# A hybrid decoder block: the two ends of its feed-forward stage rearranged

## The chip, the cores and the metric

The kernel runs on one core of one Trainium2 chip. The metric is device time in microseconds of one execution, as a median over runs. Five engines of the core appear in the profile: PE (TensorE, matmuls) with PEld (its weight loads), DVE (VectorE), ACT (ScalarE), POOL (GpSimd) and SP (SyncE, which here only issues DMAs).

## What is computed

One decoder layer on x of 512 tokens by 2048 features, all in float32. Two token mixers (block-sparse attention and a state-space group) give `mixed` (512 x 2048); then

```
x = x + mixed @ w_out                       # w_out 2048 x 2048
h2 = rms_norm(x, norm2_gain)                # x * rsqrt(mean(x^2) + eps) * gain, per token
ff = square(relu(h2 @ w_ff1))               # w_ff1 2048 x 8192
x = x + ff @ w_ff2                          # w_ff2 8192 x 2048
```

The change touches the passage from `w_out` to the feed-forward stage and that stage itself.

## The kernel before, in words

**Split products.** Each float32 operand is used as a sum of two float32r parts, high and low: ScalarE casts to the high part (`S.copy`), VectorE subtracts it from the operand (`V.tensor_sub`) for the low part. A product then takes three matmuls per tile (low x high, high x low, high x high), each 128 x 128 weights by 512 columns. Weights come by DMA on SP's queue in 512 KB loads.

**End of `w_out` (lines 802 to 824).** `panel` computes 512 output columns (a quarter, n = 0 to 3) for all four token tiles m into four PSUM banks. VectorE adds each bank, scaled, to x1[m] (line 809); ScalarE squares the result into a temporary and keeps the sum (`ssq2`, line 811). Then the quarter is transposed, 4 x 4 transposes into banks `ht` (line 819), and `scaled_split` (lines 183, 184) makes the pair h2h[n], h2l[n], without the per-token factor. After quarter 3, `rsqrt_mean` (lines 168 to 179, a chain of 14 small VectorE operations) makes that factor `rstd2`, and `token_bcast` (lines 186 to 194) spreads it over a 128 x 512 tile `rbc` by four copies `tbw` and a product with the identity into bank `tb`. `rbc` is first read in `ff1`'s eviction (line 872).

**Buffers.** `early` holds the pools of weights `wp` (28 KB per partition), temporaries `tmp` (12 KB) and PSUM `psm` (four banks for panels, one `ax`) and the three banks for transposes. They are closed at line 829; the pools opened next, `ff` in SBUF and `pff` with all eight PSUM banks, lie on the same addresses, and each of their tiles waits only for the tiles that lay there (`reuse_waits="tile"`). In `ff` are, in this order, 7 raw weight tiles of 4 KB per partition, 3 `th`, 3 `tl` of 4 KB, 9 left factors `lf` of 4 KB and 3 temporaries `ls` of 2 KB.

**The feed-forward loop (lines 849 to 986).** The 8192 hidden columns are 16 blocks b of 512. `ff1(b, r)` is the first product, a generator of 32 steps: two halves hf of 256 hidden columns, 16 steps k each, six matmuls `f` a step (lines 864 to 866); every fourth step loads and splits one `w1` tile (lines 845, 846). Step k reads h2h[k // 4]. At the end of a half VectorE applies relu and `rbc`, ScalarE squares (lines 872, 873). `left(r)` makes from r the seven left factors of a Strassen-Winograd product with two-by-two quarters a11, a12, a21, a22 (first index: token half, second: hidden half hf, so a11 and a21 come from hf = 0): each factor a cast and a subtraction (lines 884, 885), with sums s1 to s4 between. `ff2(b, lf)` is the second product: two column halves n of 1024 outputs, seven products of 12 matmuls `g` each (lines 930 to 934) in the order 1, 5, 6, 2, 7, 3, 4; each splits its right operand (line 846), which before products 5, 6, 7, 4 VectorE makes in place (lines 945, 949, 955, 961), and adds its bank to x1 (line 940). Banks X, Y, Z carry running sums over several products. In the last block the 16 output DMAs of line 967 follow.

**What sets the order.** The loop interleaves by hand: after each product of `ff2(b)` two or three steps of `ff1(b + 1)` are written, `drain(f1, 2 + (i % 7 in (1, 4)))`, 16 for each n, so that in each n one hf passes; in the last block there is no `ff1`. Ahead of the loop `drain(ff1(0, r))` runs alone. The framework (`schedule_with_timeline_sim=True`) then orders each engine's instructions from the written order, from `hi()` (high priority: splits, evictions, x1 additions) and from a timeline of its own; an engine works through its instructions in that order. SP's queue is such an order too: a load waits for a free raw tile, and what is queued behind it waits as well.

Of the kernel before, what the change touches and what calls it, by code (L numbers as in the profile page):

```python
# [45 lines left out]
def hybrid_block_kernel(ctx, tc, x, norm1_gain, w_in, q_norm_gain, k_norm_gain,  # L46
# [26 lines left out]
    def ax(name):  # L73
        return psm.tile([P, 512], F32, name=name, tag="ax", bufs=1)
# [13 lines left out]
    def tq(name, shape=(P, 512)):  # L88
        return tmp.tile(list(shape), F32, name=name, tag="tq", bufs=4)
# [93 lines left out]
        S.activation(dh, src, AF.Copy, scale=gain)  # L183
        V.scalar_tensor_tensor(dl, src, gain, dh.bitcast(F32), op0=ALU.mult, op1=ALU.subtract)

    def token_bcast(dst, col4):

        ps = ax("tb")
        for m in range(4):
            w = tq("tbw", (P, P))  # L190
            V.tensor_scalar(w, col4[:, m:m + 1].to_broadcast([P, P]), 1.0, None,
                            op0=ALU.mult)
            PE.matmul(ps[:, m * P:(m + 1) * P], w, ident, start=True, stop=True)
        V.tensor_copy(dst, ps)
# [606 lines left out]

    ssq2 = const.tile([P, 4, 4], F32, name="ssq2")
    h2h, h2l = [], []
    for n in range(4):
        ps = panel(w_out, 0, 8, n * 512, aact, True)
        for m in range(4):
            with hi():
                xs = x1[m][:, n * 512:(n + 1) * 512]
                V.scalar_tensor_tensor(xs, ps[m], rstda[:, m:m + 1], xs, op0=ALU.mult, op1=ALU.add)
            junk = t2("junk")  # L810
            S.activation(junk, xs, AF.Square, accum_out=ssq2[:, m, n:n + 1])
        h_, l_ = page(f"h2h{n}", F32R), page(f"h2l{n}", F32R)
        h2h.append(h_)
        h2l.append(l_)
        for k in range(4):
            ps = aux("ht", "tx")
            for m in range(4):
                c0 = n * 512 + k * P
                PE.transpose(ps[:, m * P:(m + 1) * P], x1[m][:, c0:c0 + P], ident)
            scaled_split(h_[:, k, :], l_[:, k, :], ps, g2[:, 4 * n + k:4 * n + k + 1])  # L820
    V.tensor_reduce(ssx, ssq2, axis=AX.X, op=ALU.add)
    rstd2 = const.tile([P, 4], F32, name="rstd2")
    rsqrt_mean(rstd2, ssx, D, [P, 4])
    token_bcast(rbc, rstd2)

    early.close()
    NB = FF // 512  # L830
    with tc.tile_pool(name="ff", bufs=2, reuse_waits="tile") as fp, \
            tc.tile_pool(name="pff", bufs=8, space=PSUM, reuse_waits="tile") as pp:

        def bank(name):
            return pp.tile([P, 512], F32, name=name, tag="pb", bufs=8)
# [37 lines left out]
                        S.activation(q, q, AF.Square)  # L873
                yield

        def left(r):

            v = r.rearrange("p (j q) (i t) -> p j q i t", j=2, i=2)
            a11, a12, a21, a22 = v[:, 0, :, 0, :], v[:, 1, :, 0, :], v[:, 0, :, 1, :], v[:, 1, :, 1, :]
            out = {}  # L880

            def put(n, src):
                t = fp.tile([P, 2, 2, 256], F32R, name="lf", tag="lf", bufs=9)
                S.copy(t[:, 0], src)
                V.tensor_sub(t[:, 1], src, t[:, 0].bitcast(F32))  # L885
                out[n] = t

            def tmp_(n):
                return fp.tile([P, 2, 256], F32, name=n, tag="ls", bufs=3)

            put(1, a11)
            s1 = tmp_("s1")
            V.tensor_add(s1, a21, a22)
            put(5, s1)
            s2 = tmp_("s2")
            V.tensor_sub(s2, s1, a11)
            put(6, s2)
            put(2, a12)
            s3 = tmp_("s3")
            V.tensor_sub(s3, a11, a21)  # L900
            put(7, s3)
            s4 = tmp_("s4")
            V.tensor_sub(s4, a12, s2)
            put(3, s4)
            put(4, a22)
            return out

        def ff2(b, lf):

            for n in range(2):  # L910
                c = [slice(n * 1024 + e * 512, n * 1024 + (e + 1) * 512) for e in range(2)]
                w = {}
                for j, e in ((0, 0), (0, 1), (1, 1), (1, 0)):
                    w[j, e] = raw_tile("w2", (P, 2, 512))
                    k0 = 4 * b + 2 * j
                    nc.sync.dma_start(
                        out=w[j, e],
                        in_=w_ff2[k0 * P:(k0 + 2) * P, c[e]].rearrange("(k p) c -> p k c", p=P))
                b11, b12, b21, b22 = w[0, 0], w[0, 1], w[1, 0], w[1, 1]
                X, Y, Z = ([None, None] for _ in range(3))  # L920

# [19 lines left out]

                product(1, b11, X, True, [(0, 0)])
                yield
                with hi():
                    V.tensor_sub(b11, b12, b11)
                product(5, b11, Z, True, [(1, 1)])
# [1 line left out]
                with hi():  # L948
                    V.tensor_sub(b11, b22, b11)
                product(6, b11, X, False, [(0, 1)])  # L950
                yield
                product(2, b21, Y, True, [(0, 0)])
                yield
                with hi():
                    V.tensor_sub(b12, b22, b12)
# [17 lines left out]
                n = n and n - 1  # L973

        r = page("r")
        drain(ff1(0, r))
        for b in range(NB):
            lf = left(r)
            if b + 1 < NB:
                r = page("r")  # L980
                f1 = ff1(b + 1, r)
            else:
                f1 = iter(())
            for i, _ in enumerate(ff2(b, lf)):
                drain(f1, 2 + (i % 7 in (1, 4)))
            drain(f1)


# [28 lines left out]
```

## Time and profile before

| | |
|---|---|
| median of 3 runs | 2176.16 us (2175.5 to 2178.85) |
| the profiled execution | 2173.75 us |
| its span, first to last instruction | 2171.8 us |
| busy share of the span: PE, PEld | 98%, 79% |
| busy share: DVE, ACT, POOL | 70%, 38%, 9% |
| mean granted TensorE clock | 0.992 |
| DMA | 213.51 MB, mean 98 GB/s |

A row of the profile names the kernel's line, the engine, the operation, its output and inputs, and their shapes; an idle time ahead of it stands in brackets with what ended it. Matmuls overlap and their ends are modelled, so that their durations may add up to more than the time that passes.

### The profile page before, as it was taken

To read this page: it belongs to the slowest core of one execution; us is meant where nothing else is said; L and a number is where in the kernel's file an instruction comes from. 1 tells how busy PE (TensorE), PEld (TensorE's weight loads), DVE (VectorE), ACT (ScalarE), POOL (GpSimd) and SP (SyncE) were. 2 spreads that over 40 slices of the span, in tenths; PEclk is the share of its full clock that TensorE was granted. 3 is DMA by queue.
4 is the path that set the end of the run, shared out by engine and by line. 5 is a ranking of instruction groups with operands and counts; after the bars stand their busy time and mean duration, and the time that the engine had idled before them with its cause. 6 is when DMAs were issued, how large, how long until landed. Compare 5 with 4: busy or idle time off the path is not lost.

```text
span 2171.8 us, 26019 instructions
## 1 busy us (share of the span) xinstructions
PE 2118.2 (98%) x9893; PEld 1711.0 (79%) x9893; DVE 1522.5 (70%) x2526; ACT 821.2 (38%) x1297; POOL 200.2 (9%) x291
## 2 busy tenths in 40 slices
PE   8899899999999998999999999999999999999997
PEld 6677677777778887888888888888888888888886
DVE  6889992444584444677777777777778778778768
ACT  5233443444454243333333333333333334334333
POOL 1487640000020000000000000000000000000000
PEclk9999999999999999999999999999999999999999
DMA  6332232222132223233333333333333333333332
GB/s 194 107 95 81 88 88 83 65 67 69 49 126 79 95 80 126 87 98 97 107 107 97 107 101 99 111 98 97 116 97 97 116 98 97 110 104 97 107 107 88
DMA packets 149613, 213.51 MB, mean 98 GB/s; under 512 B 15672, under 2 KB 82320, under 8 KB 148976
## 3 DMA queue, kind: packets, MB, share of 16 engines
q1 hardware_dynamic: 136240, 201.36, 29.5%
q10 hardware_dynamic: 12416, 8.92, 1.4%
q0 software_dynamic: 832, 1.57, 0.3%
q8 instruction: 78, 1.28, 0.3%
q14 instruction: 47, 0.39, 0.1%
HBM read 204.54 MB, written 7.27 MB: 98 GB/s over the span
## 4 chain that ended last, share of the span: by engine, by line
PE 86%; DVE 9%; issue 2%; POOL 1%; DMA 1%; ACT 1%; SPq 0%; ACTq 0%; DVEq 0%; POOLq 0%
PE f L864 11%; PE f L866 11%; PE f L865 11%; PE g L930 9%; PE g L934 9%; PE g L932 9%; PE mm L133 6%; PE mm L132 6%; PE mm L134 6%; PE sps L685 2%; PE ops L701 1%; PE mm L136 1%; PE mm L137 1%; PE mm L138 1%; DVE tl L846 1%
## 5 line engine op out<-in xcount | busy, mean ns | idle before, releaser
L845 ACT CAST th<-w 128x1024 fp32r<-128x1024 f32 x352 | 368.8, 1054 | 790.5 <-PE g L934 599.7
L846 DVE TENSOR_TENSOR tl<-w,th 128x1024 fp32r<-128x1024 f32 x352 | 425.8, 1221 | 69.3 <-ACT th L845 68.9
L940 DVE TENSOR_TENSOR x<-x,g 128x512 f32<-128x512 f32 x448 | 299.6, 684 | 248.8 <-PE g L934 248.4
L864 PE MATMUL f<-h2h,tl 128*128 128x512 f32 x1024 | 401.5, 392 | 3.5 <-DVE tl L846 2.1
L865 PE MATMUL f<-h2l,th 128*128 128x512 f32 x1024 | 399.6, 390 | 0.0
L866 PE MATMUL f<-h2h,th 128*128 128x512 f32 x1024 | 399.5, 390 | 0.0
L932 PE MATMUL g<-tl,lf 128*128 128x512 f32 x896 | 349.5, 390 | 0.0
L934 PE MATMUL g<-th,lf 128*128 128x512 f32 x896 | 349.3, 390 | 0.0
L930 PE MATMUL g<-th,lf 128*128 128x512 f32 x896 | 333.9, 391 | 7.2 <-DVE lf L885 6.1
L111 DVE TENSOR_TENSOR wl<-raw,wh 128x512 fp32r<-128x512 f32 x208 | 150.4, 727 | 174.8 <-ACT wh L110 174.4
L864 PEld LDWEIGHTS f<-h2h,tl 128*128 128x128 f32 x1024 | 192.8, 188 | 49.3 <-DVE tl L846 7.4
L866 PEld LDWEIGHTS f<-h2h,th 128*128 128x128 f32 x1024 | 192.9, 188 | 40.3
L865 PEld LDWEIGHTS f<-h2l,th 128*128 128x128 f32 x1024 | 192.9, 188 | 39.6
L110 ACT CAST wh<-raw 128x512 fp32r<-128x512 f32 x208 | 128.4, 620 | 205.7 <-PE mm L134 133.6
L930 PEld LDWEIGHTS g<-th,lf 128*128 128x128 f32 x896 | 168.5, 188 | 43.3 <-DVE lf L885 6.5
L934 PEld LDWEIGHTS g<-th,lf 128*128 128x128 f32 x896 | 168.7, 188 | 35.0
L932 PEld LDWEIGHTS g<-tl,lf 128*128 128x128 f32 x896 | 168.7, 188 | 35.0
L133 PE MATMUL mm<-wl,xh 128*128 128x512 f32 x384 | 154.7, 403 | 0.0
L132 PE MATMUL mm<-wh,xl 128*128 128x512 f32 x384 | 154.4, 403 | 0.0
L134 PE MATMUL mm<-wh,xh 128*128 128x512 f32 x384 | 153.9, 401 | 0.0
L133 PEld LDWEIGHTS mm<-wl,xh 128*128 128x128 f32 x384 | 72.8, 190 | 21.6 <-issue 7.5
L132 PEld LDWEIGHTS mm<-wh,xl 128*128 128x128 f32 x384 | 72.8, 190 | 18.8 <-issue 4.0
(337 smaller groups left out, 2632.9 us busy)
## 6 DMA issues: line engine op xcount, KB each, us to landing
w<-in_w_ff_dram SPq DMA_DIRECT2D x256, 512.0 KB, 4.0
raw<-in_w_in_dram SPq DMA_DIRECT2D x64, 512.0 KB, 3.8
raw<-in_w_out_dram SPq DMA_DIRECT2D x32, 512.0 KB, 3.6
x<-in_x_dram SPq DMA_DIRECT2D x7, 1024.0 KB, 11.5
m<-kp ACTq DMA_DIRECT2D x16, 256.0 KB, 3.3
raw<-in_w_glu_dram SPq DMA_DIRECT2D x8, 512.0 KB, 3.6
out_dram<-x SPq DMA_DIRECT2D x16, 256.0 KB, 2.2
ud<-sy ACTq DMA_DIRECT2D x8, 256.0 KB, 2.1
```

Of the source, the lines that this page charges most:

```text
L132: PE.matmul(ps[m], xl[:, ms], wh, start=st, stop=False)
L133: PE.matmul(ps[m], xh[:, ms], wl, start=False, stop=False)
L134: PE.matmul(ps[m], xh[:, ms], wh, start=False, stop=sp)
L845: S.copy(th, src)
L846: V.tensor_sub(tl, src, th.bitcast(F32))
L864: PE.matmul(ps[m], wl[:, k % 4, ms], xh_, start=k == 0, stop=False)
L865: PE.matmul(ps[m], wh[:, k % 4, ms], xl_, start=False, stop=False)
L866: PE.matmul(ps[m], wh[:, k % 4, ms], xh_, start=False, stop=k == 15)
L930: PE.matmul(ps[t], al_, th[:, q, :], start=first and q == 0, stop=False, skip_group_check=True)
L932: PE.matmul(ps[t], ah_, tl[:, q, :], start=False, stop=False, skip_group_check=True)
L934: PE.matmul(ps[t], ah_, th[:, q, :], start=False, stop=q == 1, skip_group_check=True)
L940: V.tensor_add(xs, xs, ps[t])
```

## The change

Entry: `h2_quarter` holds a quarter's transposes and splits; quarter 3's call, the sum of squares, `rstd2` and the broadcast are written between steps of `ff1(0)` (behind steps 8 and 11), with five banks taken ahead for them. The Squares write into `rbc`. Left factors: `left` becomes `left_first` (factors 1 and 7), written behind the first product of n = 1 (i = 7) for the following block, and `left_rest`; factors and their temporaries move to a pool `ffl`, opened ahead of `ff`. Products in the order 1, 2, 5, 6, 7, 3, 4, `w2` loads ordered to match. Last block, n = 0: a plain product of 96 matmuls, for which a factor 8 (a21) is added, with its output DMAs right behind each addition.

```
--- before.py
+++ after.py
@@ -183,11 +183,11 @@
         S.activation(dh, src, AF.Copy, scale=gain)
         V.scalar_tensor_tensor(dl, src, gain, dh.bitcast(F32), op0=ALU.mult, op1=ALU.subtract)
 
-    def token_bcast(dst, col4):
-
-        ps = ax("tb")
+    def token_bcast(dst, col4, bank=ax, buf=tq):
+
+        ps = bank("tb")
         for m in range(4):
-            w = tq("tbw", (P, P))
+            w = buf("tbw", (P, P))
             V.tensor_scalar(w, col4[:, m:m + 1].to_broadcast([P, P]), 1.0, None,
                             op0=ALU.mult)
             PE.matmul(ps[:, m * P:(m + 1) * P], w, ident, start=True, stop=True)
@@ -801,34 +801,35 @@
 
     ssq2 = const.tile([P, 4, 4], F32, name="ssq2")
     h2h, h2l = [], []
+
+    def h2_quarter(n, bank):
+        for k in range(4):
+            ps = bank("ht")
+            for m in range(4):
+                c0 = n * 512 + k * P
+                PE.transpose(ps[:, m * P:(m + 1) * P], x1[m][:, c0:c0 + P], ident)
+            scaled_split(h2h[n][:, k, :], h2l[n][:, k, :], ps, g2[:, 4 * n + k:4 * n + k + 1])
+
     for n in range(4):
         ps = panel(w_out, 0, 8, n * 512, aact, True)
         for m in range(4):
             with hi():
                 xs = x1[m][:, n * 512:(n + 1) * 512]
                 V.scalar_tensor_tensor(xs, ps[m], rstda[:, m:m + 1], xs, op0=ALU.mult, op1=ALU.add)
-            junk = t2("junk")
-            S.activation(junk, xs, AF.Square, accum_out=ssq2[:, m, n:n + 1])
+            S.activation(rbc, xs, AF.Square, accum_out=ssq2[:, m, n:n + 1])
         h_, l_ = page(f"h2h{n}", F32R), page(f"h2l{n}", F32R)
         h2h.append(h_)
         h2l.append(l_)
-        for k in range(4):
-            ps = aux("ht", "tx")
-            for m in range(4):
-                c0 = n * 512 + k * P
-                PE.transpose(ps[:, m * P:(m + 1) * P], x1[m][:, c0:c0 + P], ident)
-            scaled_split(h_[:, k, :], l_[:, k, :], ps, g2[:, 4 * n + k:4 * n + k + 1])
-    V.tensor_reduce(ssx, ssq2, axis=AX.X, op=ALU.add)
-    rstd2 = const.tile([P, 4], F32, name="rstd2")
-    rsqrt_mean(rstd2, ssx, D, [P, 4])
-    token_bcast(rbc, rstd2)
+        if n < 3:
+            h2_quarter(n, lambda name: aux(name, "tx"))
 
 
 
 
     early.close()
     NB = FF // 512
-    with tc.tile_pool(name="ff", bufs=2, reuse_waits="tile") as fp, \
+    with tc.tile_pool(name="ffl", bufs=3, reuse_waits="tile") as flp, \
+            tc.tile_pool(name="ff", bufs=2, reuse_waits="tile") as fp, \
             tc.tile_pool(name="pff", bufs=8, space=PSUM, reuse_waits="tile") as pp:
 
         def bank(name):
@@ -873,36 +874,46 @@
                         S.activation(q, q, AF.Square)
                 yield
 
-        def left(r):
-
+        def quarters(r):
             v = r.rearrange("p (j q) (i t) -> p j q i t", j=2, i=2)
-            a11, a12, a21, a22 = v[:, 0, :, 0, :], v[:, 1, :, 0, :], v[:, 0, :, 1, :], v[:, 1, :, 1, :]
-            out = {}
-
-            def put(n, src):
-                t = fp.tile([P, 2, 2, 256], F32R, name="lf", tag="lf", bufs=9)
-                S.copy(t[:, 0], src)
-                V.tensor_sub(t[:, 1], src, t[:, 0].bitcast(F32))
-                out[n] = t
-
-            def tmp_(n):
-                return fp.tile([P, 2, 256], F32, name=n, tag="ls", bufs=3)
-
-            put(1, a11)
-            s1 = tmp_("s1")
+            return v[:, 0, :, 0, :], v[:, 1, :, 0, :], v[:, 0, :, 1, :], v[:, 1, :, 1, :]
+
+        def factor(src):
+
+            t = flp.tile([P, 2, 2, 256], F32R, name="lf", tag="lf", bufs=9)
+            S.copy(t[:, 0], src)
+            V.tensor_sub(t[:, 1], src, t[:, 0].bitcast(F32))
+            return t
+
+        def ltmp(n, shape=(P, 2, 256)):
+            return flp.tile(list(shape), F32, name=n, tag="ls", bufs=3)
+
+        def left_first(r):
+
+            a11, a12, a21, a22 = quarters(r)
+            out = {1: factor(a11)}
+            s3 = ltmp("s3")
+            V.tensor_sub(s3, a11, a21)
+            out[7] = factor(s3)
+            return out
+
+        def left_rest(r, out, last):
+            a11, a12, a21, a22 = quarters(r)
+            out[2] = factor(a12)
+            if last:
+                out[8] = factor(a21)
+                out[4] = factor(a22)
+            s1 = ltmp("s1")
             V.tensor_add(s1, a21, a22)
-            put(5, s1)
-            s2 = tmp_("s2")
+            out[5] = factor(s1)
+            s2 = ltmp("s2")
             V.tensor_sub(s2, s1, a11)
-            put(6, s2)
-            put(2, a12)
-            s3 = tmp_("s3")
-            V.tensor_sub(s3, a11, a21)
-            put(7, s3)
-            s4 = tmp_("s4")
+            out[6] = factor(s2)
+            s4 = ltmp("s4")
             V.tensor_sub(s4, a12, s2)
-            put(3, s4)
-            put(4, a22)
+            out[3] = factor(s4)
+            if not last:
+                out[4] = factor(a22)
             return out
 
         def ff2(b, lf):
@@ -910,12 +921,30 @@
             for n in range(2):
                 c = [slice(n * 1024 + e * 512, n * 1024 + (e + 1) * 512) for e in range(2)]
                 w = {}
-                for j, e in ((0, 0), (0, 1), (1, 1), (1, 0)):
+                for j, e in ((0, 0), (1, 0), (0, 1), (1, 1)):
                     w[j, e] = raw_tile("w2", (P, 2, 512))
                     k0 = 4 * b + 2 * j
                     nc.sync.dma_start(
                         out=w[j, e],
                         in_=w_ff2[k0 * P:(k0 + 2) * P, c[e]].rearrange("(k p) c -> p k c", p=P))
+                if b == NB - 1 and n == 0:
+                    for e in range(2):
+                        ws = [split(w[j, e], (P, 2, 512)) for j in range(2)]
+                        for m in range(4):
+                            ps = bank("g")
+                            ts = slice(m % 2 * P, (m % 2 + 1) * P)
+                            for j in range(2):
+                                a = lf[(1, 2)[j] if m < 2 else (8, 4)[j]]
+                                th, tl = ws[j]
+                                for q in range(2):
+                                    PE.matmul(ps, a[:, 1, q, ts], th[:, q, :], start=j + q == 0, stop=False)
+                                    PE.matmul(ps, a[:, 0, q, ts], tl[:, q, :], start=False, stop=False)
+                                    PE.matmul(ps, a[:, 0, q, ts], th[:, q, :], start=False, stop=j + q == 2)
+                            with hi():
+                                xs = x1[m][:, c[e]]
+                                V.tensor_add(xs, xs, ps)
+                            nc.sync.dma_start(out=out2[m * P:(m + 1) * P, c[e]], in_=xs)
+                    continue
                 b11, b12, b21, b22 = w[0, 0], w[0, 1], w[1, 0], w[1, 1]
                 X, Y, Z = ([None, None] for _ in range(3))
 
@@ -941,6 +970,8 @@
 
                 product(1, b11, X, True, [(0, 0)])
                 yield
+                product(2, b21, Y, True, [(0, 0)])
+                yield
                 with hi():
                     V.tensor_sub(b11, b12, b11)
                 product(5, b11, Z, True, [(1, 1)])
@@ -948,8 +979,6 @@
                 with hi():
                     V.tensor_sub(b11, b22, b11)
                 product(6, b11, X, False, [(0, 1)])
-                yield
-                product(2, b21, Y, True, [(0, 0)])
                 yield
                 with hi():
                     V.tensor_sub(b12, b22, b12)
@@ -973,9 +1002,20 @@
                 n = n and n - 1
 
         r = page("r")
-        drain(ff1(0, r))
+        f1 = ff1(0, r)
+        held = [bank("ht") for _ in range(4)] + [bank("tb")]
+        drain(f1, 8)
+        h2_quarter(3, lambda name: held.pop(0))
+        drain(f1, 3)
+        V.tensor_reduce(ssx, ssq2, axis=AX.X, op=ALU.add)
+        rstd2 = const.tile([P, 4], F32, name="rstd2")
+        rsqrt_mean(rstd2, ssx, D, [P, 4])
+        token_bcast(rbc, rstd2, lambda name: held.pop(0), lambda n, shape: ltmp(n, shape))
+        drain(f1, 5)
+        first = left_first(r)
+        drain(f1)
         for b in range(NB):
-            lf = left(r)
+            lf = left_rest(r, first, b == NB - 1)
             if b + 1 < NB:
                 r = page("r")
                 f1 = ff1(b + 1, r)
@@ -983,6 +1023,8 @@
                 f1 = iter(())
             for i, _ in enumerate(ff2(b, lf)):
                 drain(f1, 2 + (i % 7 in (1, 4)))
+                if i == 7 and b + 1 < NB:
+                    first = left_first(r)
             drain(f1)
 
 
```

## Rows read from the trace of the kernel before

**Rows 1.** The page: part 1; groups of part 5 (busy us, mean ns); part 6.
```profile
PE 2118.2 (98%) x9893; PEld 1711.0 (79%) x9893; DVE 1522.5 (70%) x2526; ACT 821.2 (38%) x1297; POOL 200.2 (9%) x291
...
L845 ACT CAST th<-w 128x1024 fp32r<-128x1024 f32 x352 | 368.8, 1054 | 790.5 <-PE g L934 599.7
L846 DVE TENSOR_TENSOR tl<-w,th 128x1024 fp32r<-128x1024 f32 x352 | 425.8, 1221 | 69.3 <-ACT th L845 68.9
L940 DVE TENSOR_TENSOR x<-x,g 128x512 f32<-128x512 f32 x448 | 299.6, 684 | 248.8 <-PE g L934 248.4
...
w<-in_w_ff_dram SPq DMA_DIRECT2D x256, 512.0 KB, 4.0
```
**Rows 2.** Timeline of PE, first block: start, duration (us), what.
```profile
849.08 0.39 PE L864 MATMUL f<-h2h,tl 128*128 128x512 f32 x1
...
889.20 0.39 PE L864 MATMUL f<-h2h,tl 128*128 128x512 f32 x1
```
**Rows 3.** Table by stage: length, busy us of engines (instructions), PEclk, DMA share, GB/s.
```profile
844.08:848.85 4.77, 4.77 (x12) 3.77 (x13) 2.12 (x2) 0.00 (x0) 0.00 (x0) 0.51 0.75 235
...
1050.00:2100.00 1050.00, 1048.74 (x4613) 864.78 (x4611) 795.54 (x938) 375.45 (x425) 0.00 (x0) 1.00 0.33 102
...
2128.60:2132.20 3.60, 3.59 (x9) 2.83 (x10) 3.60 (x6) 0.07 (x1) 0.00 (x0) 0.50 0.02 5
2132.20:2152.00 19.80, 19.80 (x89) 16.32 (x87) 18.98 (x25) 6.34 (x7) 0.00 (x0) 1.00 0.36 133
```
**Rows 4.** Waits of PE and PEld, 848 us on: total us, times, longest.
```profile
PE g L930 <- DVE lf L885: 6.1, 1, 6.1
...
PEld f L864 <- DVE tl L846: 7.4, 14, 0.5
```
**Rows 5.** Timeline of PE, from the last panel to the feed-forward stage.
```profile
832.61 1.55 PE L819 MATMUL ht<-ident,x 128*128 128x128 f32 x12
835.79 0.66 PE L819 MATMUL ht<-ident,x 128*128 128x128 f32 x4 [1.63 <-DVE h2l L184]
839.93 2.07 PE L193 MATMUL tb<-ident,tbw 128*128 128x128 f32 x8 [3.48 <-DVE tbw L191]
844.08 0.77 PE L864 MATMUL f<-h2h,tl 128*128 128x512 f32 x1 [2.07 <-DVE tl L846]
```
**Rows 6.** Timeline of SP's queue and of DVE, the same stretch.
```profile
829.86 14.47 SPq L857 DMA_DIRECT2D w<-in_w_ff_dram  x7
...
830.77 2.79 DVE L809 SCALAR_TENSOR_TENSOR x<-mm,rstda,x 128x512 f32<-128x512 f32 x4 [2.66 <-PE mm L134]
...
839.65 0.63 DVE L191 TENSOR_SCALAR tbw<-rstd 128x128 f32<-128x128 f32 x4
```
**Rows 7.** Timelines of PE, DVE and ACT where the last block begins.
```profile
2122.09 0.39 PE L934 MATMUL g<-th,lf 128*128 128x512 f32 x1
2128.61 0.79 PE L930 MATMUL g<-th,lf 128*128 128x512 f32 x1 [6.13 <-DVE lf L885]
...
2120.86 0.69 DVE L872 SCALAR_TENSOR_TENSOR r<-f,rbc 128x512 f32<-128x512 f32 x1
...
2127.86 1.29 DVE L885 TENSOR_TENSOR lf<-s,lf 128x512 fp32r<-128x512 f32 x2
...
2121.58 0.64 ACT L873 ACTIVATE r<-r 128x512 f32<-128x512 f32 x1 [1.10 <-DVE r L872]
...
2124.67 0.61 ACT L884 CAST lf<-s 128x512 fp32r<-128x512 f32 x1
```
**Rows 8.** Timeline of PE in the last block, between its halves.
```profile
2151.95 0.39 PE L934 MATMUL g<-th,lf 128*128 128x512 f32 x1
...
2154.68 0.40 PE L932 MATMUL g<-tl,lf 128*128 128x512 f32 x1
```
**Rows 9.** Timeline of DVE in the middle of block 14.
```profile
2083.72 0.69 DVE L885 TENSOR_TENSOR lf<-r,lf 128x512 fp32r<-128x512 f32 x1
...
2087.22 0.69 DVE L940 TENSOR_TENSOR x<-x,g 128x512 f32<-128x512 f32 x1 [1.67 <-PE g L934]
```

## The prediction

> **What bounds the kernel now.** The page's first part comes first: TensorE is busy 98% of the span, VectorE 70% [rows 1]. A busy TensorE need not be paced by itself, so I looked at the spacing of its starts. Between two L864 matmuls of the first feed-forward block there are 177 matmuls in 40.12 us, 0.2267 us each [rows 2], although each is drawn 0.39 us long: they overlap, and only starts are a price. Next the table by stage: in 1050 us of the steady blocks TensorE is busy for all but 1.3 us, at full clock [rows 3]. So the steady stage is paced by the number of matmuls, and what the change can win are the places where TensorE stands still. The list of waits names them from 848 us on: 6.1 us for a left factor, once, and 14 short waits of a weight load for `tl`, 7.4 us together and at most 0.5 us each, one in each of 14 steady blocks [rows 4]; a last one, inside the last block, comes below. Ahead of 848 us the TensorE timeline shows the entry: transposes, a wait, four more, a wait, the broadcast, a wait, and the first `f` matmul at 844.08 [rows 5]. After both long waits the granted clock is one half (1.2 GHz instead of 2.4) for 4.77 us and 3.6 us [rows 3].
>
> **Entry.** Now: the last `w_out` matmul is followed at 832.61 by the 16 transposes of quarter 3 and the 8 broadcast matmuls, and `f` starts at 844.08 [rows 5]: 11.47 us. Of the slow 4.77 us, at clock 0.51, about half is lost, 2.3 us [rows 3]. The change lets `f` start at 832.61 with what is at hand (quarters 0 to 2 cover k = 0 to 11), and puts the transposes behind step 8 and the broadcast behind step 11. Their own TensorE time remains: 12 transposes 1.3 us and four 0.4 us by their rows less the drawn overlap, so 1.7 us, and the broadcast, 2.07 us drawn on a slow clock [rows 5], between 1.0 and 2.0 us; I take 1.5, as the clock should be whole. Gain: 11.5 + 2.3 - 1.7 - 1.5 = **10.6 us**.
>
> What must be in time for that: (1) the first `w1` splits. In before seven loads go out from 829.86 on [rows 6], held by buffers that lie where `w_out`'s weights and temporaries lay. The new pool `ffl` (9 factors of 4 KB and 3 of 2 KB per partition, 42 KB) is opened first and covers these 40 KB, so `raw`, `th` and `tl` land on space left earlier; a load (4.0 us), a cast (1.05) and a subtraction (1.22) [rows 1] fit ahead of 832.61. (2) Banks: `held` takes five, which by order of opening are the panel's four and `ax`; `f` gets those of the earlier transposes. (3) Quarter 3: x1's four additions on VectorE end at 833.6 [rows 6]; step 8 ends 8 x 6 x 0.2267 = 10.9 us after the start, at 843.5. (4) The scale: the first `tbw` was made at 839.65, with quarter 3's splits mixed in [rows 6]; step 11 comes at 832.61 + 15.0 + 1.7 = 849.3. (5) `rbc` is first read at the eviction behind step 16, 6.8 us later. The Squares now write `rbc` instead of a temporary, same cost, on ScalarE in order; three `tbw` buffers for four copies cost a short wait at most. Each has 6 us or more of cover; if `tbw` were later than 849.3, the whole TensorE stream would stand behind it, and `f`'s splits behind that.
>
> Here a rule speaks against the change. The rows show no `f` matmul ahead of the broadcast, though nothing in the broadcast feeds matmuls [rows 5]. The Trainium skill (PSUM — Partial Sum Buffer, Engine vs sequencer instructions) says that matmuls start and complete in program order; by that rule work put between steps stops every step behind it when late, and the sum would lose each such microsecond. This is part of the second rival.
>
> **The end of the last block.** Now: TensorE stops after 2122.09 until 2128.61 [rows 7]; less one spacing 6.3 us. Then 3.6 us at half clock, 1.8 us lost [rows 3]. The chain is the last eviction on VectorE (2120.86), its Square (2121.58 + 0.64), the sum s1, its cast (2124.67), other VectorE work, the subtraction from 2127.86 on [rows 7]. Product 5 stood behind that. In the n = 0 half VectorE is busy 18.98 of 19.80 us [rows 3]; being late, it stops TensorE again: 2151.95 to 2154.68 holds five spacings, 1.13 us, and so 1.6 us of waiting [rows 8].
>
> After: the plain product needs factors 1, 2, 8, 4. Factors 1 and 8 read only the first half of r, in place long before. Only 2 and 4 read the second half: Square's end 2122.2, cast 0.61, subtraction 0.69 [rows 7], about 2123.7 with the hand-overs. From 2119.6 (where block 15's first product starts now, 12 spacings ahead of 2122.3) the parts with factors 1 and 8, 4 x 6 matmuls, give 5.4 us of cover, to 2125.0. So the wait goes, if the framework puts these parts first; if it keeps the written order (m = 0, then its second part), cover is six matmuls, to 2121.0, and 2.7 us of wait remain. I take 0 and keep 2.7: the framework already mixes `f` and `g` freely where one is late. The plain half has 96 matmuls instead of 84: +12 x 0.2267 = 2.7 us. VectorE's side falls by 3 splits and 4 subtractions of 128x1024 and 6 additions, 7 x 1.22 + 6 x 0.68 = 12.6 us by [rows 1] (a subtraction has the shape of a `tl`), and rises by one factor (0.69); so the stop at 2152 should go too: splits for n = 1 can be made while the plain half runs. Next to be late there are the three `th` buffers. Gain: 6.3 + 1.8 + 1.6 - 2.7 = **7.0 us**. The eight output DMAs of that half wait for additions on SP's queue; the last `w2` load of n = 1, should it queue behind one, is needed only at product 6, some 30 us on. The end (last addition, last DMA) is as before.
>
> A sentence on the price of the 12: by LDWEIGHTS time, which the Trainium skill (Perfetto Trace Analysis, Identifying the Most-Contended Engine) prefers to the drawn matmul time, the nearest row is 864.78 us for 4611 loads [rows 3], 0.188 each, so 2.3 us for 12 instead of 2.7; starts decide here, and the sum would change by 0.4.
>
> **Steady blocks.** `left_first` moves two casts, two factor subtractions and s3 from the block's start to its middle, behind `i == 7`; product 2 comes second, products 5 to 4 follow, and the `w2` loads are reordered to match. Nothing is added. Factor 1 is made mid-block already, and VectorE waits 1.67 us for TensorE right after it [rows 9]: room for the 2 x 0.65 that are new there. Product 2 now needs factor 2 at 24 matmuls (5.4 us) behind the last `f`, against about 4.1 us for its chain. I price this at 0; bounds: the 14 short waits go, -7.4 us [rows 4]; or the moved work reaches TensorE (third rival).
>
> **Sum.** 10.6 + 7.0 = 17.6 us. The profiled execution took 2173.75 us (span 2171.8), 2.4 under the median of 2176.16; I subtract from the median: **2158.6 us**. A difference under about 0.2% (4.4 us) can't be told from none for this kernel.
>
> **Rivals.** *First, the short waits go as well*: 17.6 + 7.4, 2151.2 us. For: the order of splits changes in each half. Against: three `th` buffers and the same number of splits. Chance 0.1. *Second, an end keeps half its wait*: at the entry, loads still behind `w_out`'s buffers (4.0 + 1.05 + 1.22 from 829.9 on, so 3.6 us behind 832.6, and the clock's 2.3) or a late broadcast; or at the last block the 2.7, with the clock's 1.8 and 1.6 again. Each costs about 6 us: 2164.6; both, 2170.6. For: VectorE and ScalarE work in the order given to them, and `hi()` splits go first. Chance 0.2. *Third, slower*: in the middle of each block the three moved VectorE operations stand ahead of a `tl` that a matmul wants. Place: behind `i == 7`, 15 times. Price: up to 0.65 + 0.65 + 0.69, 2.0 us a block, 30 us, so 2188.6; it decides from 17.6 / 15 = 1.2 us a block on. For: TensorE has waited for a `tl` in 14 blocks, so there is little slack [rows 4]. Against: that wait is 0.5 us at most, and VectorE idles beside it [rows 9]. Chance 0.08, of which 0.05 slower and 0.03 within the bound. That the code wouldn't do what it says (`f` still behind quarter 3 because of the banks) is the second rival's upper case.
>
> **Numbers.** Forecast 0.62, first rival 0.1, second 0.2, third 0.08. The range reaches from the first rival, less what is uncertain in it, to the second with one end: 2152 to 2166; outside are both ends late and the third rival. Faster 0.91, same 0.04, slower 0.05.
>
> **What would show it.** Right: the first `f` start within 1 us of the last `w_out` start, granted clock 1.0 throughout, ht and tb rows lying between L864-line rows; the last block without a TensorE wait over 1 us, 180 `g` matmuls in it instead of 168; a steady block still at its 360 x 0.2267 = 81.6 us and the short wait. Wrong: a wait of `f` or `ht` for VectorE in 832 to 880; a wait for `lf` after the last `f` with a clock of 0.5 behind it; a steady block above 83 us with `f` or `g` waiting for `tl` near the block's middle.

## The result, and the profile after

The changed kernel takes **2156.53 us** (median of four runs, 2154.98 to 2157.2) against 2176.73 for the kernel before in the same series: 20.2 us less, ratio 0.9905, interval [0.9893, 0.9916]. Forecast was 2158.6 with a range of 2152 to 2166. The total came out 2 us from the forecast, but two of its three terms were well off.

To see that, I cut the feed-forward stage of both traces at starts of matmuls: *entry* from the last `w_out` matmul to block 0's last `f`, *steady* from there to block 15's last `f` (15 blocks), *last block* from there to the last `g`. In us:

| | last `w_out` | entry | steady | last block | rest | span |
|---|---|---|---|---|---|---|
| before | 832.38 | 57.27 | 1229.72 | 47.82 | 4.63 | 2171.82 |
| after | 834.42 | 46.28 | 1224.00 | 43.79 | 4.63 | 2153.11 |
| difference | +2.04 | **-10.99** | **-5.72** | **-4.03** | 0 | -18.71 |
| predicted | 0 | -10.6 | 0 | -7.0 | 0 | -17.6 |

The first column is not the change's: all but 0.1 of the 2.04 us is there at the first `w_out` matmul (619.60 before, 621.55 after), and from that one to the last `w_out` takes 212.8 and 212.9 us. In the profiles of the experiments below the last `w_out` matmul starts anywhere from 833.5 to 837.6. That is why stages, not totals, are compared from here on, each read from one profiled execution; they repeat far better (a steady block of the changed kernel takes 81.60 us, 15 times out of 15). The three stages together are 20.7 us shorter.

The page after, parts 1 and 5, as in [rows 1]: 12 more matmuls, 3 fewer splits, 14 fewer x additions on their line, for which line 945 makes 8.

```profile
PE 2113.7 (98%) x9905; PEld 1711.1 (79%) x9905; DVE 1517.7 (70%) x2514; ACT 818.6 (38%) x1295; POOL 199.6 (9%) x291
...
L846 ACT CAST th<-w 128x1024 fp32r<-128x1024 f32 x349 | 361.7, 1054 | 644.9 <-PE g L963 467.3
L847 DVE TENSOR_TENSOR tl<-w,th 128x1024 fp32r<-128x1024 f32 x349 | 425.9, 1221 | 63.0 <-ACT th L846 63.0
L969 DVE TENSOR_TENSOR x<-x,g 128x512 f32<-128x512 f32 x434 | 294.0, 684 | 241.3 <-PE g L963 240.7
```

The busy shares are those of before to a per cent: nothing in them tells that 20 us went. The table by stage does (length, busy us of PE, PEld, DVE, ACT, POOL, granted clock, DMA share, GB/s), beside [rows 3]: block 0 and the 15 steady blocks run without a gap at full clock; the start of the last block has one, of 4.78 - 3.10 us, and goes on at full clock.

```profile
834.64:880.70 46.06, 46.06 (x217) 38.45 (x215) 22.06 (x41) 13.93 (x21) 0.00 (x0) 1.00 0.22 67
880.70:2104.70 1224.00, 1224.00 (x5402) 1013.51 (x5401) 934.17 (x1093) 437.34 (x495) 0.00 (x0) 1.00 0.33 104
2104.70:2109.48 4.78, 3.10 (x14) 2.25 (x13) 4.78 (x7) 4.73 (x7) 0.00 (x0) 1.00 0.00 0
...
2109.48:2114.00 4.52, 4.52 (x20) 3.73 (x21) 4.52 (x8) 1.24 (x2) 0.00 (x0) 1.00 0.01 5
```

The waits of PE and PEld from 848 us on, as in [rows 4]: the line of 14 short waits for `tl` is gone, the one for a left factor is 1.7 us instead of 6.1, and a small one for `tl` remains in the last block.

```profile
PE g L940 <- DVE lf L885: 1.7, 1, 1.7
PE g L961 <- DVE tl L847: 0.5, 1, 0.5
...
PEld g L940 <- DVE lf L885: 2.1, 1, 2.1
PEld g L961 <- DVE tl L847: 1.3, 2, 0.9
```

The timeline of PE at the entry, against [rows 5]: the first `f` is one spacing behind the last `w_out` matmul, the transposes and the broadcast lie between `f` rows, and none has a wait in front.

```profile
834.42 0.39 PE L134 MATMUL mm<-wh,ah 128*128 128x512 f32 x1
834.64 0.39 PE L865 MATMUL f<-h2h,tl 128*128 128x512 f32 x1
...
845.53 1.91 PE L810 MATMUL ht<-ident,x 128*128 128x128 f32 x16
...
851.37 0.83 PE L193 MATMUL tb<-ident,tbw 128*128 128x128 f32 x6
...
856.40 0.38 PE L193 MATMUL tb<-ident,tbw 128*128 128x128 f32 x2
```

Timelines of SP's queue and of VectorE there, against [rows 6]: the first three `w1` loads go out at 742 (before, the first of them at 818.73, and seven from 829.86 on); three `tbw` copies are made at 839.67, the fourth waits for a buffer until 851.79, which TensorE doesn't feel because its last two broadcast matmuls come at 856.40.

```profile
741.75 1.47 SPq L858 DMA_DIRECT2D w<-in_w_ff_dram  x3
...
839.67 0.50 DVE L191 TENSOR_SCALAR tbw<-rstd 128x128 f32<-128x128 f32 x3
...
851.79 0.23 DVE L191 TENSOR_SCALAR tbw<-rstd 128x128 f32<-128x128 f32 x1 [1.12 <-PE tb L193]
```

Timelines of PE, VectorE and ScalarE where the last block begins, against [rows 7]: the last `f` starts at 2104.70, then come twelve `g` matmuls (to 2107.41), then nothing until the first subtraction of line 885.

```profile
2107.41 0.39 PE L942 MATMUL g<-th,lf 128*128 128x512 f32 x1
2109.48 0.50 PE L940 MATMUL g<-th,lf 128*128 128x512 f32 x1 [1.68 <-DVE lf L885]
...
2105.27 0.68 DVE L873 SCALAR_TENSOR_TENSOR r<-f,rbc 128x512 f32<-128x512 f32 x1
2105.87 2.35 DVE L847 TENSOR_TENSOR tl<-w,th 128x1024 fp32r<-128x1024 f32 x2
2108.14 0.68 DVE L907 TENSOR_TENSOR s<-r 128x512 f32<-128x512 f32 x1
2108.74 1.28 DVE L885 TENSOR_TENSOR lf<-r,lf 128x512 fp32r<-128x512 f32 x2
...
2104.71 2.01 ACT L846 CAST th<-w 128x1024 fp32r<-128x1024 f32 x2 [1.18 <-PE g L963]
2106.62 0.63 ACT L874 ACTIVATE r<-r 128x512 f32<-128x512 f32 x1
2107.28 1.66 ACT L884 CAST lf<-r 128x512 fp32r<-128x512 f32 x3
```

Read the chain from the eviction (2105.27): the Square could follow at 2106 but stands behind two `th` casts until 2106.62; three casts of factors follow at once, among them factor 8's, though it needs only the first half of r; the sum s1 stands ahead of the subtractions. So factor 8 arrives with factor 2, and the cover for factor 2 (the matmuls that can run while it is made) is the 12 with factor 1 instead of 24.

### The profile page after: what moved, and what is told of

Its sections match the earlier page's. It is cut to its first block, busy times and chain, and to the rows that moved or that the text cites. A ratio compares the mean times of both kernels' runs of the same rounds, so it can differ in the third digit from the quotient of the medians.

```text
span 2153.1 us, 26096 instructions
## 1 busy us (share of the span) xinstructions
PE 2113.7 (98%) x9905; PEld 1711.1 (79%) x9905; DVE 1517.7 (70%) x2514; ACT 818.6 (38%) x1295; POOL 199.6 (9%) x291
## 4 chain that ended last, share of the span: by engine, by line
PE 87%; DVE 8%; issue 1%; DMA 1%; POOL 1%; ACT 1%; SPq 0%; ACTq 0%; DVEq 0%; POOLq 0%
PE f L865 11%; PE f L866 11%; PE f L867 11%; PE g L961 9%; PE g L963 9%; PE g L959 9%; PE mm L133 6%; PE mm L132 6%; PE mm L134 6%; PE sps L685 2%; PE ops L701 2%; PE mm L136 1%; DVE wl L111 1%; PE mm L137 1%; PE mm L138 1%
## 5 line engine op out<-in xcount | busy, mean ns | idle before, releaser
L846 ACT CAST th<-w 128x1024 fp32r<-128x1024 f32 x349 | 361.7, 1054 | 644.9 <-PE g L963 467.3
L969 DVE TENSOR_TENSOR x<-x,g 128x512 f32<-128x512 f32 x434 | 294.0, 684 | 241.3 <-PE g L963 240.7
L961 PE MATMUL g<-tl,lf 128*128 128x512 f32 x868 | 337.9, 389 | 0.5 <-DVE tl L847 0.5
L963 PE MATMUL g<-th,lf 128*128 128x512 f32 x868 | 337.7, 389 | 0.0
L959 PE MATMUL g<-th,lf 128*128 128x512 f32 x868 | 320.0, 389 | 0.0
L961 PEld LDWEIGHTS g<-tl,lf 128*128 128x128 f32 x868 | 162.9, 188 | 35.0 <-DVE tl L847 1.3
L959 PEld LDWEIGHTS g<-th,lf 128*128 128x128 f32 x868 | 163.0, 188 | 33.8
L963 PEld LDWEIGHTS g<-th,lf 128*128 128x128 f32 x868 | 162.9, 188 | 33.8
L874 ACT ACTIVATE r<-r 128x512 f32<-128x512 f32 x64 | 40.0, 628 | 146.5 <-DVE r L873 146.5
```

The source lines that it names most:

```text
L846: S.copy(th, src)
L959: PE.matmul(ps[t], al_, th[:, q, :], start=first and q == 0, stop=False, skip_group_check=True)
L961: PE.matmul(ps[t], ah_, tl[:, q, :], start=False, stop=False, skip_group_check=True)
L963: PE.matmul(ps[t], ah_, th[:, q, :], start=False, stop=q == 1, skip_group_check=True)
L969: V.tensor_add(xs, xs, ps[t])
```

## The experiments

Eight kernels in two series, each beside the kernel before. The same cut for all (us; the kernel before has a median of 2178.01 in the series of the first four, 2178.61 in that of the others, and the ratio is against it):

| | entry | steady | last block | median | ratio |
|---|---|---|---|---|---|
| e1: before + order of products | 57.51 | 1224.00 | 50.55 | 2174.54 | 0.998 [0.9971, 0.9989] |
| e2: before + early factors | 57.26 | 1229.75 | 48.00 | 2177.88 | 1.000 [0.999, 1.0009] |
| e3: before + entry | 46.28 | 1229.60 | 48.59 | 2163.16 | 0.9934 [0.9919, 0.9949] |
| e4: after - plain product | 46.28 | 1224.00 | 46.46 | 2158.41 | 0.991 [0.9895, 0.9925] |
| e5: after, factor 8 early | 46.28 | 1224.00 | 41.83 | 2153.05 | 0.9885 [0.987, 0.990] |
| e6: after, pool order swapped | 53.88 | 1224.00 | 43.78 | 2162.05 | 0.9929 [0.9914, 0.9944] |
| e7: after, entry work later | 46.28 | 1224.00 | 43.79 | 2156.5 (one run) | |
| e8: after + VectorE work | 46.28 | 1224.00 | 43.78 | 2157.33 | 0.99 [0.9882, 0.9917] |

### e1: the order of products alone

```
-                for j, e in ((0, 0), (0, 1), (1, 1), (1, 0)):
+                for j, e in ((0, 0), (1, 0), (0, 1), (1, 1)):
...
                 product(1, b11, X, True, [(0, 0)])
                 yield
+                product(2, b21, Y, True, [(0, 0)])
+                yield
```

(and product 2 taken out behind product 6)

> The kernel before with the new order of products (1, 2, 5, 6, 7, 3, 4) and of the w2 loads, nothing else. What is disputed is where 5.7 us of the steady stage went (last f matmul of block 0 to last f of block 15: 1229.72 us before, 1224.00 after). Theory: product 2, which needs no subtraction ahead, standing second gives the splits more lead, so the short waits for tl go: steady stage 1224 to 1225, total about 0.997 of before. Rival (the early factors did it): steady stage stays 1229 to 1230, total 1.000. Entry as before, 57.3 us from the last panel matmul to the last f of block 0, by both.

Steady came to 1224.00, every block 81.6: the short waits go with the order of products and `w2` loads alone. The timeline of PE at the last block shows what this order costs without the early factors and the new order of making them:

```profile
2121.42 0.39 PE L934 MATMUL g<-th,lf 128*128 128x512 f32 x1
2129.90 0.80 PE L930 MATMUL g<-th,lf 128*128 128x512 f32 x1 [8.09 <-DVE lf L885]
```

Factor 2 is now wanted second, but still made behind 5 and 6, so the last block is 2.7 us longer than before. Where the short wait of before came from can be read in a steady block of the kernel before (timelines of ScalarE, VectorE and PEld): a cast sits idle until a `g` matmul gives back its `th` buffer (1113.30), its subtraction stands behind an x addition until 1115.04, and the `f` weight load that reads the result waits for 0.53 us.

```profile
1113.30 1.06 ACT L845 CAST th<-w 128x1024 fp32r<-128x1024 f32 x1 [6.88 <-PE g L934]
...
1114.44 0.69 DVE L940 TENSOR_TENSOR x<-x,g 128x512 f32<-128x512 f32 x1 [0.45 <-PE g L934]
1115.04 1.22 DVE L846 TENSOR_TENSOR tl<-w,th 128x1024 fp32r<-128x1024 f32 x1
...
1116.31 0.19 PEld L864 LDWEIGHTS f<-h2h,tl 128*128 128x128 f32 x1 [0.53 <-DVE tl L846]
```

That the new order removes it is shown; by which step of the schedule (the splits' sequence, the load order, or both) was not taken apart.

### e2: the early factors alone

```
+                if i == 7 and b + 1 < NB:
+                    first = left_first(r)
```

(with `left_first` and `left_rest` as in the change, the old order of products, the old entry)

> The kernel before with factors 1 and 7 made behind the first product of n = 1, old order of products, nothing else. Theory (the order of products removed the short waits): steady stage stays at 1229 to 1230, and the 6.1 us wait at the last block stays too, since product 5, still second, needs a sum of the second half of r: total 0.999 to 1.000. Rival (the early factors did it): steady stage 1224 to 1225, total 0.997. Third (moved VectorE work reaches TensorE): steady stage above 1231.

Nothing moved: the short waits are all there, and so is the wait of the last block (waits of PEld and PE in this kernel):

```profile
PEld f L864 <- DVE tl L846: 7.7, 15, 0.5
...
PE g L940 <- DVE lf L884: 6.1, 1, 6.1
```

So the early factors neither help nor hurt by themselves; the moved VectorE work doesn't reach TensorE. In the last block they count only together with the order: order alone +2.7 us, early alone +0.2, both, with the new entry (e4), -1.4.

### e3: the entry alone

```
+        f1 = ff1(0, r)
+        held = [bank("ht") for _ in range(4)] + [bank("tb")]
+        drain(f1, 8)
+        h2_quarter(3, lambda name: held.pop(0))
+        drain(f1, 3)
...
```

(the change's entry and its pool `ffl`; `left`, the order and the last block as before)

> The kernel before with the entry alone: quarter 3 and the broadcast between steps of the first product, the pool of factors opened first; old factors, old order of products, no plain product. Theory: entry 46 to 47 us instead of 57.3, and all of it stays to the end, since TensorE is paced by its matmuls from there on: total 0.995. Rival: part is given back in the first block, because the first product then waits for factor 1, which is made only when the first product's last step is done: entry 46 to 47, steady stage 2 us longer than 1229.7, total 0.996.

The entry gains its whole 11.0 us, and the steady blocks give none of it back (1229.60 for 1229.72). The last block is 0.8 us longer: behind the same standstill, 6.51 us between starts in both kernels, the granted clock is at its lower level for 5.3 us here and for 3.6 before.

### e4: the change without its plain product

```
-                if b == NB - 1 and n == 0:
+                if False:
...
-            lf = left_rest(r, first, b == NB - 1)
+            lf = left_rest(r, first, False)
```

> The kernel after with the seven products in the last block too. The last block (last f to last g matmul) took 47.8 us before and 43.8 after. Theory: VectorE paces the last block when it has seven splits, four subtractions and fourteen additions in each half; without the plain product it takes 45 to 47 us with waits for tl or th inside, total 1 to 3 us above the kernel after. Rival: the wait for a left factor at its start was all that mattered; then it takes 168 x 0.2267 = 38.1 us and a wait of about 2, some 40 us, and the kernel is 3.5 us faster than after: the plain product costs its 12 matmuls for nothing.

The last block takes 46.46, so the plain product is worth 2.67 us: its 12 extra matmuls (2.7 us) are more than paid for by the stops that go. This rests on the stages; the medians of the two kernels are too near to tell them apart. Without it waits of 1.2 us for a `th` and 0.9 for `tl` are in the block, as the theory had it. The timeline of PE shows what else stays in: the wait for the factor, then matmuls that soon slow down.

```profile
2106.81 0.39 PE L963 MATMUL g<-th,lf 128*128 128x512 f32 x1
2110.08 0.50 PE L959 MATMUL g<-th,lf 128*128 128x512 f32 x1 [2.88 <-DVE lf L885]
```

### e5: factor 8 made early

```
-        def left_first(r):
+        def left_first(r, last=False):
...
+            if last:
+                out[8] = factor(a21)
...
-                    first = left_first(r)
+                    first = left_first(r, b + 2 == NB)
```

(and taken out of `left_rest`)

> Changed kernel with factor 8 of the last block made in the middle of the block before (with factors 1 and 7) instead of at its end. Theory (the 2.06 us at the start of the last block are missing cover: only the 12 matmuls with factor 1 are ready, and factor 8 is made together with factor 2): now 24 matmuls, 5.4 us, are ready, the gap goes to below 0.5 us, the last block takes about 41.8 us instead of 43.8, and the time falls by about 2 us against the changed kernel. Rival (the order of matmuls is fixed with factor 2's parts right behind the first 12, or factor 2 itself comes later than 5.4 us behind the last f): the gap stays at 2 us or shrinks by the 0.6 us of one cast at most.

The gap is gone: between the last `f` and 2137 no two matmul starts are more than 0.3 us apart, and of the waits of PE one line is left, the small `tl` one:

```profile
PE g L962 <- DVE tl L847: 0.4, 1, 0.4
```

The last block is 41.83, 1.96 us less, against 180 x 0.2267 = 40.8 for its matmuls alone. This is the fastest of the kernels here: median 2153.05. Its interval against the kernel before overlaps the change's own, so the 2 us rest on the traces: from the last `w_out` matmul to the last `g` 1312.10 us, in the changed kernel 1314.07.

### e6: the pool of factors behind `ff`

```
-    with tc.tile_pool(name="ffl", bufs=3, reuse_waits="tile") as flp, \
-            tc.tile_pool(name="ff", bufs=2, reuse_waits="tile") as fp, \
+    with tc.tile_pool(name="ff", bufs=2, reuse_waits="tile") as fp, \
+            tc.tile_pool(name="ffl", bufs=3, reuse_waits="tile") as flp, \
```

> Changed kernel with the pool of left factors opened behind the pool ff instead of ahead of it, so that the raw, th and tl tiles lie again where w_out's weights and temporaries lay. Theory (the prediction's point 1: the place of the pool is what frees the first w1 loads): the loads go out at about 830 instead of 742, the first f waits for load, cast and subtraction, so that it starts 3 to 7 us behind the last w_out matmul, and the next matmuls have half the clock; entry 50 to 54 us instead of 46.3, total 4 to 8 us up. Rival (the loads are early in any case, since other tiles became free long before): f starts right behind the last w_out matmul, entry 46.3 us, no change.

Two swapped lines cost 7.6 us. The timelines of SP's queue and PE: the loads go out some 80 us later, and the first `f` waits for its `tl`, 5.41 us behind the last `w_out` matmul (836.74).

```profile
823.08 19.40 SPq L858 DMA_DIRECT2D w<-in_w_ff_dram  x8
```

```profile
836.74 0.39 PE L134 MATMUL mm<-wh,ah 128*128 128x512 f32 x1
842.15 0.80 PE L865 MATMUL f<-h2h,tl 128*128 128x512 f32 x1 [5.02 <-DVE tl L847]
```

The load itself is not what takes the time. The first goes out at 823.08, and the eight take 3.8 to 8.1 us each to land, so that it is there by 831.2 at the latest. The timelines of ScalarE and VectorE show what comes then: ScalarE stands idle until the first Square of the last panel, the cast of the first `w1` tile comes only behind the four Squares, and its subtraction between the small operations of `rsqrt_mean`. In the changed kernel the first cast is made at 746.00. Why the later loads put the casts there in ScalarE's order was not taken apart.

```profile
835.97 0.64 ACT L819 ACTIVATE rbc<-x 128x512 f32<-128x512 f32 x1 [4.29 <-DVE x L818]
...
838.86 1.97 ACT L846 CAST th<-w 128x1024 fp32r<-128x1024 f32 x2
...
840.87 1.23 DVE L847 TENSOR_TENSOR tl<-w,th 128x1024 fp32r<-128x1024 f32 x1
```

Behind the wait the clock is at its lower level for 4.8 us, by the table of two stretches:

```profile
842.15:846.95 4.80, 4.80 (x11) 3.80 (x12) 3.27 (x10) 0.05 (x1) 0.00 (x0) 0.50 1.09 349
846.95:890.62 43.67, 43.67 (x206) 36.38 (x205) 18.12 (x21) 11.99 (x15) 0.00 (x0) 1.00 0.31 99
```

5.41 - 0.23 = 5.2 us of wait and 2.4 of slow clock. The medians differ by less: 2162.05 is 4.7 us above e8 of the same series, and 5.5 above the changed kernel in the first; the profiled execution was the slowest of its four.

### e7: the entry's work later

```
-        drain(f1, 8)
+        drain(f1, 11)
...
-        drain(f1, 3)
+        drain(f1, 4)
...
-        drain(f1, 5)
+        drain(f1, 1)
```

> Changed kernel with quarter 3's transposes written behind step 11 instead of 8 of the first product and the broadcast behind step 15 instead of 11: both as late as the data allow. Theory (TensorE works in its fixed order, and what counts is the distance between transposes and the first matmul that reads their splits): with one step, 1.4 us, between them TensorE waits 0.5 to 2.5 us for the first split of quarter 3; the broadcast costs nothing more, as rbc is read by VectorE alone and banks are free; entry 47 to 49 us. Rival (the framework puts the transposes at the same place whatever the written order): entry 46.3 us and transposes again at 845.

Neither held. The transposes did move, to 15.0 us behind the first `f` instead of 10.9 (the broadcast, written four steps later, came only 1.4 us later, at 854.26, and its last two matmuls 2.5), but TensorE doesn't wait. The timelines of PE, ScalarE and VectorE say why:

```profile
851.14 1.91 PE L810 MATMUL ht<-ident,x 128*128 128x128 f32 x16
852.80 0.48 PE L865 MATMUL f<-h2h,tl 128*128 128x512 f32 x1
...
851.77 2.42 ACT L183 ACTIVATE h2h<-ht,vt 128x512 fp32r<-128x512 f32 x4 [3.47 <-PE ht L810]
...
852.50 2.07 DVE L184 SCALAR_TENSOR_TENSOR h2l<-ht,vt,h2h 128x512 fp32r<-128x512 f32 x3 [2.93 <-ACT h2h L183]
```

The first split starts as soon as the first four transposes are out, while twelve more run; its low part is there at about 853.25, before the step between (852.80, six matmuls) has passed. I had counted from the end of the transposes. One step of distance is enough here.

### e8: more VectorE work in the middle of a block

```
                 if i == 7 and b + 1 < NB:
                     first = left_first(r)
+                    for _ in range(3):
+                        d = fp.tile([P, 512], F32, name="dum", tag="dum", bufs=2)
+                        V.tensor_sub(d, r[:, 0, :], r[:, 1, :])
```

> Changed kernel with three additional subtractions of 128x512 on VectorE (operands in place, result unused) behind i = 7 in each of the 15 blocks, about 2 us of VectorE a block more at the place where the moved factors are made. Prices the third rival. Theory (VectorE has slack in the middle of a block): steady stage stays within 3 us of 1224.0 us. Rival (the work reaches TensorE): up to 2 us a block, steady stage 1239 to 1254 us, with f or g waiting for tl near the blocks' middle.

The groups of the steady stage show the 45 operations done, 29.5 us of them, and the stage stays at 1224.00:

```profile
L1030 DVE TENSOR_TENSOR dum<-r 128x512 f32<-128x512 f32 x45 | 29.5, 683 | 0.0
```

Two more microseconds a block on top of the moved work cost nothing.

## Why the prediction was right in sum and wrong in two terms

**Entry: right, -10.99 for -10.6.** By its own terms: from the last `w_out` matmul to the first `f` 11.70 us before and 0.23 after (11.47; predicted 11.5); slow clock 45.57 - 191 x 0.2267 = 2.27 (2.3); transposes and broadcast together now cost 46.28 - 192 x 0.2267 = 2.75 (predicted 1.7 + 1.5). Point (1) was the one that mattered: e6 shows that the place of the pool decides, at a price of 7.6 us where the second rival had 3.6 + 2.3. That rival's working is not what e6 shows, though: it let load, cast and subtraction follow each other from 829.9 on, but in the kernel before the first `w1` load goes out at 818.73, ahead of the seven in [rows 6], and its cast comes at 837.07, behind the Squares and quarter 3's splits (timelines of SP's queue and ScalarE). What is late, there and in e6, is the place of the cast and the subtraction in the order of ScalarE and VectorE, not the load.

```profile
818.73 16.65 SPq L857 DMA_DIRECT2D w<-in_w_ff_dram  x7
...
837.07 1.03 ACT L845 CAST th<-w 128x1024 fp32r<-128x1024 f32 x1
```

Points (3) to (5) held with more room than needed: e7 moved the transposes by 4.1 us and the broadcast by 1.4 to 2.5 at no cost. The rule weighed there (the Trainium skill, PSUM — Partial Sum Buffer, Engine vs sequencer instructions: matmuls start and complete in program order) did not come to a price: no piece written between the steps was late in any run here, so what a late one would stop was not seen. The converse was, in e6, and agrees with the rule: quarter 3's x additions end at 837.91, yet its transposes stay behind the late `f` and come at 855.45.

**Steady blocks: wrong, -5.72 for 0.** The step "I price this at 0" failed. The first rival, at 0.1, was the case: the short waits went. Its argument against ("three `th` buffers and the same number of splits") counted the splits and not where they fall: the wait came from one cast that waited for one `g` product to give back its buffer, and from a subtraction behind an x addition (the rows under e1), and with the new order this place is gone. e1 shows that the order of products and loads does it alone, e2 that the early factors don't; which part of the order does it stays open. The size is 14 x 0.41 = 5.7 us; the bound of 7.4 added up waits of weight loads, of which 0.53 us each is drawn but TensorE's starts lose 0.41.

**Last block: mis-sized, -4.03 for -7.0.** Before, the block took 47.82 - 168 x 0.2267 = 9.7 us more than its matmuls; the prediction let all of that go (6.3 + 1.8 + 1.6) and paid 2.7 for 12 matmuls, which it does (12 x 0.2267). What failed is "I take 0" for the wait for factor 2: 2.06 - 0.23 = 1.8 us of it remained, between the two ends 0 and 2.7, and 1.1 us of short stops was left, most of it in the second half (starts 0.84 us apart instead of 0.23 at 2140.03, and a few of 0.34 and 0.35), where the term 1.6 had been taken as gone. The reason was in the kept end but not seen exactly: the prediction asked whether the framework puts the parts with factors 1 and 8 first, and took factor 8 as there "long before" because its input is. It is made in `left_rest`, though, with factor 2, and its cast and subtraction come when that one's do. The framework did put ready parts first, but only the 12 matmuls with factor 1, 2.7 us, were ready, and factor 2 came 4.6 us behind the first of them (2104.92 to 2109.48) where the prediction had 4.1 (2119.6 to 2123.7). e5 moves factor 8 and the wait is gone. No slow clock followed (granted clock 1.00), so 1.8 of the predicted gains came in full.

**The third rival, slower, is out.** e2 puts the moved work into the old kernel and e8 doubles it in the new one; a steady block stays where it was both times.

So 0.4 us at the entry and 5.7 in the steady blocks made up for 3.0 at the end. The forecast was near by luck: errors of opposite sign made up for each other, and the sum itself was wrong.

## What to carry to other kernels

A short wait that recurs in every block is one place in the order of the work: find the operation that waited for a buffer, and ask of a changed order whether that place still exists, rather than whether the amount of work is the same. When an operand is to be covered by others that are "ready", see when the instructions that make it are issued, not when their input exists; making it where its input first exists was worth 2 us here. And when a stage opens new pools on old addresses, what lies on which old tile decides when its first loads go out, and with that where the framework puts the work on them in the engines' orders: two swapped lines were 7.6 us.

## What was not expected of the hardware

What followed a standstill of TensorE differed. Behind 2.06 us between starts in the changed kernel the granted clock stayed at 1.00; behind 3.27 us in e4 six matmuls ran at 0.97 and the next eight at 0.50, as its table of stretches shows; behind 5.41 us in e6 the lower level was there with the first matmul.

```profile
2110.08:2111.40 1.32, 1.32 (x6) 1.04 (x6) 1.32 (x2) 0.16 (x1) 0.00 (x0) 0.97 0.00 0
2111.40:2114.38 2.98, 2.98 (x8) 2.30 (x7) 2.98 (x5) 1.66 (x3) 0.00 (x0) 0.50 0.00 0
```

So the price of a wait is not only its length: in e4 the eight slow matmuls lost about 2.98 - 8 x 0.2267 = 1.2 us more. The other thing is that the stages ahead of the feed-forward stage end anywhere within some 5 us (832.4 to 837.6) from profile to profile. No kernel here changes what lies ahead of `w_out`, and all of the spread is there at its first matmul (619.6 to 624.8); the cause stays open.
